# Hybrid encoder block on one core: the first four key tiles projected together behind a run-up of ten matmuls, the first weight chunk and the last store in halves

## The chip, the core and the metric

The kernel runs on one core of a Trainium2 chip. A core has five engines, each with its own instruction list, which it works through in order: TensorE (PE in the profile) multiplies matrices, VectorE (DVE) and ScalarE (ACT) do elementwise work and reductions and can read the accumulators, GpSimd (POOL) does elementwise work on the main on-chip memory, and SyncE (SP) issues transfers. DMA engines move data between the large memory and the on-chip memory. The engines wait for one another through semaphores. PE writes its results to accumulators in a small memory of its own (PSUM). The metric is the time of one execution in microseconds on the device.

## The reference

One layer of an encoder on 1024 positions of 1024 channels, in float32. The parts that matter here come first:

```python
h = rms_norm(x, norm1_g[l])
z = h @ w_in[l]
a, gate, q, k, v = jnp.split(z, splits, axis=-1)
conv_out = conformer_conv(a, gate, ...)            # a * sigmoid(gate), depthwise conv of width 31, LayerNorm, SiLU
q = rms_norm(q.reshape(B, S, N_HEADS, HEAD_DIM), q_norm_g[l])
k = rms_norm(k.reshape(B, S, N_HEADS, HEAD_DIM), k_norm_g[l])
attn_out = neighbourhood_attention(q, k, v, rpb[l])
x = x + jnp.concatenate([conv_out, attn_out], axis=-1) @ w_out[l]
h = rms_norm(x, norm2_g[l])
x = x + (jax.nn.silu(h @ w_gate[l]) * (h @ w_up[l])) @ w_down[l]
```

The key part of `z` is 512 channels wide, eight heads of 64; `a` and `gate` are 512 channels each.

## The kernel before

Every matrix product is made exact enough with three products of a faster kind. An operand is split into a high part (a rounded copy) and a low part (what the rounding left), and `mac` (L110) runs three matmuls into one accumulator: high by high (L112), then the two mixed products (L113 and L114). A weight chunk of 128 x 1024 is split by `split` (L103): ACT casts the high part (L104), and DVE or POOL subtracts for the low part (L108). Weights come through a ring of three raw buffers (`R`); `issue` starts the transfer of the next chunk on SP, `take` and `take_parts` split one, the latter in parts that the caller orders. The first four chunks are `wk0` to `wk3`, the key weights, each holding two of the eight K steps. Then come the GLU chunks, `ag10` (gate, channel block 0) and `ag00` (its value) first. The low parts of the `wk` chunks are made by DVE where `take_parts` is called, those of the `ag` chunks by POOL.

The activations come as transposed x in pieces `xt` of two K steps. `h_split` scales one K step by `norm1_g` and splits it into `hT`; for the first half of the positions (tiles 0 to 3 of 128 positions) it works on 256 columns at a time, `FIRST` for tiles 0 and 1 and `SECOND` for tiles 2 and 3. The factor of the RMS norm is not applied there: it is a number for each position, computed from x itself (`load_x`) by `stats1`, and multiplied in later. `stats1` of an even tile squares and sums on ACT, of an odd tile on DVE; both end with a square root on ACT and a reciprocal on DVE.

The key projection: tiles 0 and 1 are projected together, K step by K step, as the chunks arrive, with the splits of the next pair of K steps between them. The `SECOND` splits follow, then `stats1` of tiles 0 and 1, then tile 2 alone (`project`, 24 matmuls), `stats1` of tiles 2 and 3, the split of `ag10` (`take(1, False)`), and tile 3 alone. Each finished tile goes through `head_post`: a square on ACT, a sum over each head on DVE, a square root on ACT, and the scaling on DVE (`head_sq`, `head_scale`). Then PE transposes the result (`head_T`, L390) and ACT copies it to `kT` (L397). Work of this kind waits in `pend` until the next tile's matmuls have been written out, so it runs beside them; the transposes wait in `woven`, from which one entry is taken after each K step. After the key tiles PE transposes the four factors to a row (`r_rows`, L289), and `glu_step` follows for the gate and value of channel block 0.

The order on each engine is the order in which the program writes the instructions; no scheduler moves them. There are four accumulators of 512 columns for the projections (`mm`) and two for transposes (`tp`).

At the end the down projection finishes its four last tiles one after the other. For each, DVE adds the accumulator to a partial result (L1203) and ACT issues the store (`store`, L1180), 256 KB each.

Of the kernel before, what the change touches and what calls it, by code (L numbers as in the profile page):

```python
# [9 lines left out]
OP = mybir.AluOpType  # L10
PSUM = bass.MemoryType.PSUM

P = 128
D = 1024
S = 1024
KB = D // P
# [51 lines left out]
def build(ctx, tc, a):  # L68
    nc = tc.nc
    pe, act, dve, pool = nc.tensor, nc.scalar, nc.vector, nc.gpsimd  # L70
# [5 lines left out]
    def T(tag, shape, bufs, name, dt=F32):  # L76
        return sb.tile(shape, dt, tag=tag, bufs=bufs, name=name)

    def G(name, dt=F32):
        return T("G", [P, 1024], 22, name, dt)  # L80

    def R(name):
        return T("R", [P, 1024], 3, name)

    def H(name, dt=F32):
        return T("H", [P, 4096], 6, name, dt)

    def ST(name, dt=F32):
        return T("st", [P, 512], 5, name, dt)

    def SM(name, n=8):
        return T("sm", [P, 8], 16, name)[:, :n]

    def mm(name):
        return ps.tile([P, 512], F32, tag="mm", bufs=4, name=name)

    def tp(name):
        return ps.tile([P, 512], F32, tag="tp", bufs=2, name=name)
# [11 lines left out]
    def mac(acc, l, r, start, stop):  # L110
        (lh, ll), (rh, rl) = l, r
        pe.matmul(acc, lh, rh, start=start, stop=False, skip_group_check=True)  # L112
        pe.matmul(acc, lh, rl, start=False, stop=False, skip_group_check=True)  # L113
        pe.matmul(acc, ll, rh, start=False, stop=stop, skip_group_check=True)  # L114


    woven = []
# [16 lines left out]
    def issue():  # L134
        if pos[0] < len(chunks):
            src, name, _, _ = chunks[pos[0]]
            raws[pos[0]] = R(name + "r")
            d = raws[pos[0]]
            if len(src.shape) == 3:
                d = d.rearrange("p (k m) -> p k m", k=src.shape[1])  # L140
            nc.sync.dma_start(d, src)
            pos[0] += 1

    def take(n=1, ahead=True):
# [32 lines left out]
    wn = {n: [] for n in range(3)}  # L177
# [29 lines left out]
    hT = [[H(f"hT{h}{w}", F32R).rearrange("p (k s) -> p k s", s=512) for w in range(2)] for h in range(2)]  # L207
    x_t, xr = {}, {}
    FIRST, SECOND, ALL = slice(0, 256), slice(256, 512), slice(0, 512)

    def load_x(t):
        x_t[t] = G(f"x{t}")
        nc.sync.dma_start(x_t[t], a["x"][t * P:(t + 1) * P, :])

    def load_xt(h, kp, sl):
        if (h, kp) not in xr:
            xr[h, kp] = G(f"xt{h}{kp}").rearrange("p (k s) -> p k s", s=512)
        nc.sync.dma_start(xr[h, kp][:, :, sl], a["xt"][h, kp][:, :, sl])

    for kp in range(4):  # L220
        load_xt(0, kp, FIRST)
        if kp < 3:
            issue()
    ones = ST("ones")[:, :P]
    ident = T("ident", [P, P], 1, "ident")
    par = T("par", [P, 146], 1, "par")
# [7 lines left out]
    warm = SM("warm", 1)  # L234
    act.activation(warm, eps, AF.Sqrt)
    pool.memset(ones, 1.0)
    pool.affine_select(ident, ones, pattern=[[-1, P]], compare_op=OP.is_equal, fill=0.0,
                       base=0, channel_multiplier=1)
    qgs = T("qgs", [P, 1], 1, "qgs")
# [16 lines left out]
    def h_split(h, k, sl):  # L256
        src = xr[h, k // 2][:, k % 2, sl]
        hi, lo = [w[:, k, sl] for w in hT[h]]
        act.activation(hi, src, AF.Copy, scale=g1[:, k:k + 1])
        dve.scalar_tensor_tensor(lo, src, g1[:, k:k + 1], hi.bitcast(F32), OP.mult, OP.subtract)  # L260
# [15 lines left out]
    def stats1(t):  # L276
        ss, scale = (bn_sum if t % 2 else sq_sum)(t)
        sd = SM(f"sd1{t}", 1)
        act.activation(sd, ss, AF.Sqrt, bias=eps, scale=scale)
        dve.reciprocal(r1[:, t:t + 1], sd)  # L280
# [11 lines left out]
    def nat(n, t):  # L292
        z = mm(f"z{n}{t}")
        h, o = divmod(t * P, 512)
        for k in range(KB):
            mac(z, [q[:, k, o:o + P] for q in hT[h]],
                [q[:, (k % 2) * 512:(k % 2) * 512 + 512] for q in wn[n][k // 2]], k == 0, k == KB - 1)
            weave()
        return z
# [56 lines left out]
    def pump(n):  # L356
        for _ in range(n):
            if not next(conv, False):
                return
# [4 lines left out]
    def head_sq(n, t, z):  # L364
        sq, ss = ST(f"sq{n}{t}"), SM(f"s{n}{t}")
        r = r1[:, t:t + 1]
        if n == 1 and t < 4:
            act.activation(sq, z, AF.Square, scale=r)
            dve.tensor_reduce(ss, sq.rearrange("p (h d) -> p h d", d=HD), mybir.AxisListType.X, OP.add)
        else:  # L370
            for h in range(NH):
                act.activation(sq[:, h * HD:(h + 1) * HD], z[:, h * HD:(h + 1) * HD], AF.Square, scale=r,  # L372
                               accum_out=ss[:, h:h + 1])
        sd = SM(f"d{n}{t}")
        act.activation(sd, ss, AF.Sqrt, bias=eps, scale=1.0 / HD)
        return sd

    def head_scale(n, t, z, sd):
        r = SM(f"r{n}{t}")
        dve.reciprocal(r, sd)  # L380
        dve.tensor_scalar(r, r, r1[:, t:t + 1], None, op0=OP.mult)
        zn = ST(f"zn{n}{t}")
        dve.tensor_tensor(zn.rearrange("p (h d) -> p h d", d=HD), z.rearrange("p (h d) -> p h d", d=HD),
                          r[:, :, None].to_broadcast([P, NH, HD]), OP.mult)
        return zn
# [21 lines left out]
    pend = []  # L407
# [10 lines left out]
            pump(n_taps)  # L418
        side()

    def head_post(n, t, z):
        def f(n_taps):
            sd = head_sq(n, t, z)
            pump(2)
            zn = head_scale(n, t, z, sd)
            pump(1)
            woven.extend([lambda: None] * 7)
            woven.append(lambda: head_T(n, t, zn))
        return f

# [70 lines left out]
    def project(n, t, post):  # L501
        z = nat(n, t)
        step(post(n, t, z))

    zs = [mm(f"z1{t}") for t in range(2)]
    for kp in range(4):
        parts = []
        take_parts(parts, 2, dve)
        for j in range(2):
            h_split(0, 2 * kp + j, FIRST)  # L510
            parts[j]()
        if kp == 0:
            for q in range(4):
                load_xt(0, q, SECOND)
            load_x(0)
            load_x(1)
        if kp == 2:
            load_x(2)
            load_x(3)
        for j in range(2):  # L520
            for t in range(2):
                k = 2 * kp + j
                mac(zs[t], [q[:, k, t * P:(t + 1) * P] for q in hT[0]],
                    [q[:, j * 512:(j + 1) * 512] for q in wn[1][kp]], k == 0, k == KB - 1)
    for k in range(KB):
        h_split(0, k, SECOND)
    stats1(0)
    stats1(1)
    pend.extend(head_post(1, t, zs[t]) for t in range(2))
    project(1, 2, head_post)  # L530
    stats1(2)
    stats1(3)
    take(1, False)
    for q in range(4):
        load_xt(1, q, ALL)
    project(1, 3, head_post)
    for t in range(4, 8):
        load_x(t)
    take(1)
# [222 lines left out]
    def rows(ap, t):  # L762
        rh, cb = divmod(t, 4)
        return ap.rearrange("(h i w) d -> h i w d", h=2, w=GW)[rh, :, cb * 16:cb * 16 + 16, :]
# [231 lines left out]
    for t in range(8):  # L996
        for n in range(KB):
            woven.append(lambda fs=beside.get(t, {}).get(n, ()): [f() for f in fs])
        acc = mm(f"pk{t}")
# [10 lines left out]
    gt, bank, sl, u2, late = {}, {}, {}, {}, []  # L1010
# [131 lines left out]
    for n, (i, p) in enumerate(products):  # L1142
        if i == 0 and p in NEXT:
            s_weave(NEXT[p])
        acc = product(i, p)
# [32 lines left out]
    def store(p, t, w):  # L1178
        tok, d = {"m2": (0, 0), "m3": (0, 1), "m4": (1, 0), "m7": (1, 1)}[p]
        (nc.scalar if p == "m4" else nc.sync).dma_start(  # L1180
            rows(a["out"], 4 * tok + t)[:, :, d * 512:(d + 1) * 512], w)

    def quarter(w, o, t):
        return w[:, o + t * 512:o + t * 512 + 512]

    def finish(p, t):
        acc = (GA if p in ("m1", "m2", "m7", "m4") else GB)[t]
        if p == "m1":
            if t == 0:
                om["m1"] = H("om1")  # L1190
            (dve.tensor_copy, act.copy)[t % 2](quarter(om["m1"], 2048, t), acc)
        elif p == "m2":
            dve.tensor_tensor(res[p, t], acc, res[p, t], OP.add)
            store(p, t, res[p, t])
        elif p == "m6":
            if t == 0:
                om["u"] = H("ou")
            dve.tensor_tensor(quarter(om["u"], 0, t), acc, quarter(om["m1"], 2048, t), OP.add)
        elif p == "m5":
            dve.tensor_tensor(quarter(om["u"], 2048, t), acc, quarter(om["m1"], 2048, t), OP.add)  # L1200
        else:
            w = {"m7": quarter(om["u"], 2048, t), "m3": quarter(om["m1"], 2048, t), "m4": quarter(om["u"], 0, t)}[p]
            dve.tensor_tensor(w, acc, w, OP.add)  # L1203
            store(p, t, w)

    def add_res(p, t):
        w = {"m7": quarter(om["u"], 2048, t), "m3": quarter(om["m1"], 2048, t), "m4": quarter(om["u"], 0, t)}[p]
# [8 lines left out]
    for s, p in enumerate(SEQ):  # L1216
        for k in range(QF - 2):
            n = s * QF + k
# [34 lines left out]
```

## Time and profile before

| | |
|---|---|
| median of 3 runs | 1070.03 us (1069.66 to 1070.52) |
| profiled execution, its own time | 1070.39 us |
| span of that execution | 1068.6 us |
| PE busy | 1048.0 us (98%) |
| DVE, ACT, POOL busy | 704.9, 451.3, 383.2 us |
| moved by DMA | 144.06 MB, mean 135 GB/s |

The profile is one execution. Times in it count from the start of the span. A row of the timeline gives start, duration, engine, line, operation, what is written and read, shape, and in square brackets the idle time of the engine before it with what ended it. Matmuls are pipelined, so the duration of one is longer than the distance from one start to the next; the distance is what a matmul costs. A wait is put down to the last event that ended it. In the windows each row gives, for a stretch, the busy time of each engine with the count of its instructions, then the granted clock, the mean busy share of the DMA engines and the GB/s moved.

### The profile page before, as it was taken

The numbers are of one execution on the slowest core, as the hardware profiler recorded it, in microseconds if no ns is written. First come the engines' busy times: TensorE is split into PE (matmuls) and PEld (weight loads), VectorE is DVE, ScalarE is ACT, GpSimd is POOL, SyncE is SP. The second block draws the span as 40 slices with busy tenths as digits, with TensorE's granted clock in tenths as the row PEclk, the third lists the DMA queues.
The fourth block names the chain that finished last, engine by engine and source line by source line (L and its number), as shares of the span: only waits on it lengthen the run. The fifth ranks groups of instructions, "written<-read, shape, count | busy, mean of one in ns | idle before, by whom it ended". The sixth has DMA issues, their size and how long they took to land.

```text
span 1068.6 us, 14069 instructions
## 1 busy us (share of the span) xinstructions
PE 1048.0 (98%) x5068; PEld 849.4 (79%) x5068; DVE 704.9 (66%) x1071; ACT 451.3 (42%) x987; POOL 383.2 (36%) x301
## 2 busy tenths in 40 slices
PE   7999999989999999999999999999999999999997
PEld 6788888866667888788888888888888888888886
DVE  6778997885775347766556465564655567858873
ACT  6455357725775424542322323223232344433441
POOL 0136665513562301435444554445544300002310
PEclk9999999999999999999999999999999999999999
DMA  9426781244413422132322322333232597633641
GB/s 336 158 51 221 225 251 40 75 150 137 152 62 131 164 80 82 37 107 90 128 98 84 134 99 89 109 107 109 81 129 79 179 333 276 207 98 116 216 131 41
DMA packets 68245, 144.06 MB, mean 135 GB/s; under 512 B 12496, under 2 KB 21200, under 8 KB 67536
## 3 DMA queue, kind: packets, MB, share of 16 engines
q1 hardware_dynamic: 66336, 139.95, 38.8%
q10 hardware_dynamic: 1840, 3.22, 0.9%
q8 instruction: 40, 0.66, 0.3%
q14 instruction: 29, 0.24, 0.1%
HBM read 103.99 MB, written 44.76 MB: 139 GB/s over the span
## 4 chain that ended last, share of the span: by engine, by line
PE 89%; DVE 6%; issue 1%; ACT 1%; DMA 1%; POOL 0%; SPq 0%; DVEq 0%; POOLq 0%; ACTq 0%
PE B L113 5%; PE B L114 5%; PE B L112 5%; PE D L114 4%; PE D L112 4%; PE D L113 4%; PE A L112 3%; PE A L114 3%; PE A L113 3%; DVE cv L319 3%; PE gl L114 3%; PE gl L112 3%; PE gl L113 3%; PE z L112 2%; PE z L113 2%; PE z L114 2%
## 5 line engine op out<-in xcount | busy, mean ns | idle before, releaser
L319 DVE SCALAR_TENSOR_TENSOR cv<-u,par,cv 128x1009 f32<-128x1009 f32 (+14 forms) x92 | 117.5, 1277 | 2.5
L345 POOL TENSOR_TENSOR pa<-pa,pr 128x1022 f32<-128x1022 f32 (+5 forms) x24 | 57.5, 2398 | 51.3 <-ACT pr L344 42.8
L104 ACT CAST op<-sr 128x512 fp32r<-128x512 f32 x77 | 47.7, 619 | 51.2 <-PE B2d L114 23.3
L108 DVE TENSOR_TENSOR op<-sr,op 128x512 fp32r<-128x512 f32 x77 | 57.6, 748 | 15.9 <-ACT op L104 15.8
L1036 DVE TENSOR_TENSOR g<-B,g 128x512 f32<-128x512 f32 x22 | 15.2, 691 | 79.0 <-PE B L114 79.0
L1208 POOL TENSOR_TENSOR ou<-ou,resm 128x512 f32<-128x512 f32 x8 | 13.2, 1662 | 142.9 <-DMA resm<-xd 142.9
L1045 ACT ACTIVATE D<-D 128x512 f32<-128x512 f32 x22 | 12.8, 582 | 113.1 <-DVE D L1044 113.1
L1031 DVE TENSOR_TENSOR u<-B,g 128x512 f32<-128x512 f32 x22 | 15.2, 690 | 62.5 <-PE B L114 62.5
L104 ACT CAST op<-wd 128x512 fp32r<-128x512 f32 x66 | 40.9, 619 | 31.6 <-DVE wd L1123 18.3
L108 DVE TENSOR_TENSOR op<-wd,op 128x512 fp32r<-128x512 f32 x66 | 51.7, 783 | 2.4 <-ACT op L104 0.9
L633 POOL TENSOR_SCALAR e<-e,rs 128x288 f32<-128x288 f32 (+1 forms) x64 | 34.2, 548 | 52.8 <-DVE rs L631 42.3
L889 DVE TENSOR_TENSOR ts<-gu,ts 128x512 f32<-128x512 f32 x44 | 51.0, 1159 | 0.8
L1034 ACT ACTIVATE A<-A 128x512 f32<-128x512 f32 x20 | 11.6, 582 | 76.3 <-PE A L114 76.3
L626 ACT ACTIVATE e<-e,mx 128x288 f32<-128x288 f32 (+1 forms) x64 | 36.2, 568 | 11.4 <-DVE mx L624 11.4
L624 DVE CUSTOM_DVE_ANT_0 e<-s,tab 128x288 f32<-128x288 f32 (+1 forms) x64 | 29.9, 504 | 6.7 <-PE s L611 6.4
L889 DVE TENSOR_TENSOR ts<-gu 128x512 f32<-128x512 f32 x22 | 33.5, 1524 | 0.0
L611 PE MATMUL s<-kT,qT 64*128 64x288 f32 (+1 forms) x128 | 28.1, 499 | 4.6 <-DVE mx L624 4.6
L642 PEld LDWEIGHTS p<-ident,e 128*96 128x96 f32 (+1 forms) x192 | 20.1, 133 | 15.0 <-issue 10.4
L372 ACT ACTIVATE sq<-z,r 128x64 f32<-128x64 f32 x96 | 28.6, 334 | 2.2 <-PE z L114 2.2
L642 PE MATMUL p<-ident,e 128*96 128x128 f32 (+1 forms) x192 | 27.6, 280 | 0.6 <-DVE pT L647 0.6
L658 PE MATMUL o<-pT,vw 96*64 96x128 f32 (+1 forms) x384 | 28.0, 281 | 0.0
L344 ACT ACTIVATE pr<-u,par 128x1022 f32<-128x1022 f32 (+5 forms) x24 | 27.0, 1137 | 1.6 <-ACT vs L403 1.6
(1039 smaller groups left out, 3455.0 us busy)
## 6 DMA issues: line engine op xcount, KB each, us to landing
gu<-in_gu SPq DMA_DIRECT2D x44, 512.0 KB
sr<-sd SPq DMA_DIRECT2D x77, 256.0 KB
sd<-sd SPq DMA_DIRECT2D x22, 512.0 KB
wd<-in_wd SPq DMA_DIRECT2D x44, 256.0 KB
sd<-g SPq DMA_DIRECT2D x33, 256.0 KB
x<-in_x SPq DMA_DIRECT2D x16, 512.0 KB
xd<-x SPq DMA_DIRECT2D x8, 512.0 KB
resm<-xd SPq DMA_DIRECT2D x16, 256.0 KB
```

Of the source, the lines that this page charges most:

```text
L104: act.copy(hi, src)
L108: eng.tensor_tensor(*[w[..., sl] for w in (lo, src, hi.bitcast(F32))], OP.subtract)
L112: pe.matmul(acc, lh, rh, start=start, stop=False, skip_group_check=True)
L113: pe.matmul(acc, lh, rl, start=False, stop=False, skip_group_check=True)
L114: pe.matmul(acc, ll, rh, start=False, stop=stop, skip_group_check=True)
L319: dve.scalar_tensor_tensor(acc[:, o], uc[:, i], dwk[:, c, t:t + 1], acc[:, o], OP.mult, OP.add)
L345: pool.tensor_tensor(pa[:, o], pa[:, o], pr[:, o], OP.add)
L624: dve.tensor_tensor_reduce(out=e[:, hh], in0=ss[hh], in1=tab[rh, cb][2 * hp + hh], scale=-1.0, scalar=3.0e38, op0=OP.add, op1=OP.min, accu ...
L626: act.activation(e[:, hh], e[:, hh], AF.Exp, bias=mx, scale=-1.0, accum_out=rs[:, hh:hh + 1])
L633: pool.tensor_scalar(es[i][:, hh], es[i][:, hh], rs[:, hh:hh + 1], 1.0, op0=OP.mult, op1=OP.mult)
L642: pe.transpose(pt[:m, g * P:(g + 1) * P], es[i][:, hh, g * m:(g + 1) * m], ident)
L889: dve.tensor_tensor(o, l, r, OP.subtract)
```

## The change

- All four accumulators are taken at once: tiles 0 to 3 of the keys are projected together. For the first three chunks the order is K step by K step over the four tiles; for the last chunk each tile does both its K steps, so that the tiles finish one after the other.
- The `SECOND` halves of the transposed x are issued directly behind each `FIRST` half and its chunk, and split beside them. x tiles 0 and 1 are issued in the second round, 2 and 3 in the third.
- `stats1` of all four tiles comes before the last round's matmuls, and `head_post` of tiles 0, 1 and 2 is written out among these matmuls, with a lag of two K steps instead of seven for the transposes. Tile 3's follows in the first `glu_step`. The split of `ag10` now stands behind all this, and that of `ag00` directly behind it.
- Ten matmuls of a 128 x 128 tile of ones with itself are written ahead of the first projection, into an accumulator for transposes that nobody reads.
- The first weight chunk's transfer is issued as two transfers of 512 columns.
- The last tile's final addition and store are done in two halves of 256 columns, the first stored from SP, the second from ACT.

```diff
@@ issue
-            nc.sync.dma_start(d, src)
+            for q in (0, 1) if name == "wk0" else (slice(None),):
+                sl = slice(q * 512, q * 512 + 512) if name == "wk0" else q
+                nc.sync.dma_start(d[:, sl], src[:, sl])
@@ the first loads
         load_xt(0, kp, FIRST)
         if kp < 3:
             issue()
+        load_xt(0, kp, SECOND)
...
     pool.memset(ones, 1.0)
+
+    run_up = tp("up")
+    for _ in range(10):
+        pe.matmul(run_up[:, :P], ones, ones, start=True, stop=True)
@@ head_post
-    def head_post(n, t, z):
+    def head_post(n, t, z, lag=7):
...
-            woven.extend([lambda: None] * 7)
+            woven.extend([lambda: None] * lag)
@@ the key projection
-    zs = [mm(f"z1{t}") for t in range(2)]
+    zs = [mm(f"z1{t}") for t in range(4)]
+
+    def four(kp, j, t):
+        k = 2 * kp + j
+        mac(zs[t], [q[:, k, t * P:(t + 1) * P] for q in hT[0]],
+            [q[:, j * 512:(j + 1) * 512] for q in wn[1][kp]], k == 0, k == KB - 1)
+
     for kp in range(4):
         parts = []
         take_parts(parts, 2, dve)
         for j in range(2):
             h_split(0, 2 * kp + j, FIRST)
             parts[j]()
-        if kp == 0:
-            for q in range(4):
-                load_xt(0, q, SECOND)
-            load_x(0)
-            load_x(1)
-        if kp == 2:
-            load_x(2)
-            load_x(3)
         for j in range(2):
-            for t in range(2):
-                k = 2 * kp + j
-                mac(zs[t], [q[:, k, t * P:(t + 1) * P] for q in hT[0]],
-                    [q[:, j * 512:(j + 1) * 512] for q in wn[1][kp]], k == 0, k == KB - 1)
-    for k in range(KB):
-        h_split(0, k, SECOND)
-    stats1(0)
-    stats1(1)
-    pend.extend(head_post(1, t, zs[t]) for t in range(2))
-    project(1, 2, head_post)
-    stats1(2)
-    stats1(3)
+            h_split(0, 2 * kp + j, SECOND)
+        if kp in (1, 2):
+            load_x(2 * kp - 2)
+            load_x(2 * kp - 1)
+        if kp == 3:
+            for t in range(4):
+                stats1(t)
+        for q in range(8):
+            j, t = divmod(q, 4) if kp < 3 else (q % 2, q // 2)
+            four(kp, j, t)
+            if kp == 3 and j == 1 and t < 3:
+                head_post(1, t, zs[t], 2)(4)
+    pend.append(head_post(1, 3, zs[3], 2))
     take(1, False)
     for q in range(4):
         load_xt(1, q, ALL)
-    project(1, 3, head_post)
     for t in range(4, 8):
         load_x(t)
     take(1)
@@ finish, last product
-            dve.tensor_tensor(w, acc, w, OP.add)
-            store(p, t, w)
+            for o, q in ((0, nc.sync), (256, nc.scalar)) if (p, t) == ("m4", 3) else ((None, None),):
+                if q is None:
+                    dve.tensor_tensor(w, acc, w, OP.add)
+                    store(p, t, w)
+                else:
+                    sl = slice(o, o + 256)
+                    dve.tensor_tensor(w[:, sl], acc[:, sl], w[:, sl], OP.add)
+                    q.dma_start(rows(a["out"], 4 + t)[:, :, sl], w[:, sl])
```

## The prediction

> **What bounds the kernel now.** I read the page's busy times and chain first, then PE's waits, then the order of time on each engine for the first 60 us and the last 10. Busy time and chain say that PE is the bound:
>
> ```profile
> span 1068.6 us, 14069 instructions
> PE 1048.0 (98%) x5068; PEld 849.4 (79%) x5068; DVE 704.9 (66%) x1071; ACT 451.3 (42%) x987; POOL 383.2 (36%) x301
> PE 89%; DVE 6%; issue 1%; ACT 1%; DMA 1%; POOL 0%; SPq 0%; DVEq 0%; POOLq 0%; ACTq 0%
> ```
>
> So a gain or a loss has to show as PE time. PE's waits (engine, line, what it waited for: total, times, longest) name where it stands still:
>
> ```profile
> PE z L112 <- ACT wk0h L104: 6.5, 1, 6.5
> PE s L611 <- DVE mx L624: 4.6, 1, 4.6
> PE gl L114 <- POOL ag10l L108: 0.6, 1, 0.6
> ```
>
> The first is the front, which the change attacks; the third is the gate behind the work that is regrouped. The timeline of PE (start, duration, instruction) around both:
>
> ```profile
> 6.50 0.79 PE L112 MATMUL z<-wk0h,hT 128*128 128x512 f32 x1 [6.50 <-ACT wk0h L104]
> 7.22 0.80 PE L113 MATMUL z<-wk0l,hT 128*128 128x512 f32 x1
> 10.80 0.48 PE L112 MATMUL z<-wk0h,hT 128*128 128x512 f32 x1
> 11.12 0.40 PE L113 MATMUL z<-wk0l,hT 128*128 128x512 f32 x1
> 11.35 0.40 PE L114 MATMUL z<-wk0h,hT 128*128 128x512 f32 x1
> ...
> 30.42 0.40 PE L114 MATMUL z<-wk3h,hT 128*128 128x512 f32 x1
> 30.66 0.60 PE L390 MATMUL zt<-ident,zn 128*128 128x128 f32 x4
> 31.09 0.60 PE L289 MATMUL rb<-ident,r 128*128 128x128 f32 x4
> 31.45 0.48 PE L112 MATMUL gl<-hT,ag10h 128*128 128x512 f32 x1
> 31.77 0.39 PE L113 MATMUL gl<-hT,ag10h 128*128 128x512 f32 x1
> 32.80 0.50 PE L114 MATMUL gl<-hT,ag10l 128*128 128x512 f32 x1 [0.65 <-POOL ag10l L108]
> ```
>
> Nine matmuls start from 7.22 to 10.80 and take 3.90 us until 11.12, where the pace is then 0.227 each (11.12 to 11.35): about 1.9 us lost to a slow start. At 32.80 PE passes the gate: the low half of the first GLU weight chunk, which POOL makes. ACT and POOL show how the gate comes about:
>
> ```profile
> 4.27 0.51 ACT L259 ACTIVATE hT<-xt,par 128x256 fp32r<-128x256 f32 x1 [1.57 <-DMA xt<-in_xt]
> 5.83 0.62 ACT L104 CAST wk0h<-wk0r 128x512 fp32r<-128x512 f32 x1 [1.04 <-DMA wk0r<-in_qkv]
> 8.75 0.62 ACT L104 CAST wk1h<-wk1r 128x512 fp32r<-128x512 f32 x1 [0.77 <-DMA wk1r<-in_qkv]
> 13.67 0.62 ACT L104 CAST wk3h<-wk3r 128x512 fp32r<-128x512 f32 x1 [0.95 <-DMA wk3r<-in_qkv]
> 15.12 3.31 ACT L259 ACTIVATE hT<-xt,par 128x256 fp32r<-128x256 f32 x8
> 18.33 1.01 ACT L273 ACTIVATE j<-x 128x1024 f32<-128x1024 f32 x1
> 21.90 0.67 ACT L368 ACTIVATE sq<-z,r 128x512 f32<-128x512 f32 x1
> 23.33 0.30 ACT L375 ACTIVATE d<-s,eps 128x8 f32<-128x8 f32 x1 [0.75 <-DVE s L369]
> 25.48 0.30 ACT L375 ACTIVATE d<-s,eps 128x8 f32<-128x8 f32 x1 [1.28 <-DVE s L369]
> 25.69 1.01 ACT L273 ACTIVATE j<-x 128x1024 f32<-128x1024 f32 x1
> 29.26 1.04 ACT L104 CAST ag10h<-ag10r 128x1024 fp32r<-128x1024 f32 x1
> 30.38 2.37 POOL L108 TENSOR_TENSOR ag10l<-ag10r,ag10h 128x1024 fp32r<-128x1024 f32 x1 [29.03 <-DMA xt<-in_xt]
> ```
>
> ACT runs its list in order: statistics of x tiles 0 and 1 (18.33 to 21.90, 3.57 us), heads of key tiles 0 and 1 (21.90 to 25.69), statistics 2 and 3 (25.69 to 29.26, 3.57), the cast ag10h (29.26), then POOL's subtraction 1.12 later, and PE 2.42 after that. The chunk itself is no matter: what the cast waits for is its turn. All this is covered today by PE's 48 matmuls of key tiles 2 and 3; only 0.65 us is not.
>
> **The change, part by part.** First the front. wk0 in halves: ACT can cast its first half when 256 KB less have come. At the 333 GB/s of the row below that is about 0.75 us, bounded by 5.83 (no earlier) and 4.78 (ACT free). I take 5.1, and with 0.67 from cast to matmul as before (5.83 to 6.50) PE starts at 5.8.
>
> ```profile
> 0.78 0.21 POOL L236 MEMSET ones<- 128x128 f32 x1 [0.29 <-POOLq L1243]
> 4.00:5.00 1.00, 0.00 (x0) 0.00 (x0) 0.18 (x1) 0.51 (x1) 0.00 (x0) 1.00 0.97 333
> 20.00:21.00 1.00, 1.00 (x6) 0.84 (x5) 1.00 (x2) 0.00 (x0) 0.00 (x0) 1.00 1.04 414
> ```
>
> The ten matmuls on ones wait for the memset (0.99). The trace has none like them; a transposition of the same size is 0.11 us (30.66 to 31.09 is four), a slow 128x512 matmul 0.43, so they take 1.1 to 4.3 us and end by 5.3, on an idle PE: no cost. If they ran past 5.8 PE would start later by the excess. Their gain is 0 to 1.9 us of slow matmuls; I take it whole.
>
> The four tiles: 96 matmuls, as before. 5.8, then 0.72 to the second (6.50 to 7.22), then 95 steps of 0.227: key tile 0 is done at 24.0, tile 2 at 26.7, tile 3 at 28.1, where before it was 30.65. The x transposes' second halves now go past wk1, wk2 and wk3 on SP. wk1 comes behind 256 KB more, 0.6 us at 414 GB/s: 9.4, and its first matmul is due at 11.9, after 24 of them. wk3 comes behind 1 MB more, 2.5 us: 16.2, due at 22.8. Both are covered; a lost cover would cost the excess alone.
>
> Then the gate. In the changed program ACT's list is: all four statistics, heads 0, 1, 2, cast ag10h. The statistics start after wk3's split: 16.2 plus 1.45 (13.67 to 15.12) plus two splits of 0.41 is 18.5, about the 18.33 of before, which I keep. They also need x0, which SP now issues behind ag10: 512 KB, 1.27 us at 414 GB/s, so up to 19.6 if it had landed just in time. Four statistics are 2 x 3.57, with no overlap of the pairs, since each pair ends on ACT with a square root that waits for DVE: 25.5. That is later than key tile 0 (24.0), so the early finish of PE buys nothing here. Three heads: two took 3.79 (21.90 to 25.69), a third adds 2.15 (23.33 to 25.48): 5.94. Cast at 31.4, POOL at 32.5, PE through the gate at **35.0**. Bounds: 24.0 instead of 25.5 gives 33.5; x0 late gives 36.2.
>
> So the gate opens 2.2 us later than at 32.80. Behind it everything queues on PE in order: the rest of the GLU, and the transposes of all four key tiles, of which one set (0.43 us) stood ahead of the gate before, at 30.66: +0.43. ag00, POOL's next split, is due 24 matmuls on and is hidden. Of the waits that PE has after the gate only the 4.6 us is large, and it hangs on DVE work that starts from the GLU's results, so what PE loses at the gate passes to the end in full.
>
> New: PE has nothing to do from 28.6 (tile 3 and the four rb transposes) to ag10h's end at 32.5, and again from about 33 to 35.0. What a pause of that size does stands in the trace once:
>
> ```profile
> 237.00 1.32 PE L611 MATMUL s<-kT,qT 64*128 64x288 f32 x2 [4.61 <-DVE mx L624]
> 238.25 0.79 PE L112 MATMUL z<-w20h,hT 128*128 128x512 f32 x1
> 242.68 0.58 PE L113 MATMUL z<-w21l,hT 128*128 128x512 f32 x1
> 243.10 0.39 PE L114 MATMUL z<-w21h,hT 128*128 128x512 f32 x1
> 243.33 0.39 PE L112 MATMUL z<-w22h,hT 128*128 128x512 f32 x1
> ```
>
> After 4.61 us without work the eleven steps from 238.25 to 243.10 take 4.85 us instead of 2.5: 2.35 lost. After the 0.65 us at 32.80 nothing is lost. Pauses of 3.9 and 2 us with two matmuls between lie nearer the first; between 0 and 2.35 I take 2.2.
> The Trainium skill (TensorE: Matmul & The Clock Gate, Part 1) has it that a window of about 3.4 us without work halves the clock until a busy window has passed; the windows run free, so 3.9 us does not always hold a whole one. The trace agrees with the halving (0.43 against 0.227); by the page the price is 2.2 or 0, and the sum 1074.3 or 1072.1.
>
> Last the final store. Its rows (windows: PE, PEld, DVE, ACT, POOL busy, clock, share of DMA, GB/s):
>
> ```profile
> 1058.86 4.69 ACTq L1180 DMA_DIRECT2D out_dram<-ou  x4
> 1063.00:1064.00 1.00, 0.00 (x0) 0.00 (x0) 0.00 (x0) 0.00 (x0) 0.00 (x0) 1.00 0.51 190
> 1066.00:1067.00 1.00, 0.00 (x0) 0.00 (x0) 0.00 (x0) 0.00 (x0) 0.00 (x0) 0.50 0.48 178
> ```
>
> ACT's queue alone keeps the DMA engines half busy and drains four stores of 256 KB until about 1067. 128 KB on SP's queue instead shortens that backlog by 0.7 us at 178 GB/s; with packets half as long it could be nothing. I take 0.5. The adds in halves are hidden by the backlog.
> The Trainium skill (Trainium Kernel Development and Optimization, Key Constraints) says that issuing from several engines only saves issue time; no row shows two store queues at once. By it the tail gains nothing and the sum is 1074.8.
>
> **Sum** against the profiled execution (1070.39): +2.2 gate, +0.43 transposes, +2.2 slow matmuls, -0.5 tail: +4.3, 1074.7. The median of the runs is 0.36 lower than that execution, so 1074.3.
>
> **The rivals.**
> No slow spell: the gate opens late but PE keeps its pace. For it: the pauses are shorter than 4.61 and broken by two matmuls. +2.1: 1072.1.
> The gate hardly moves: statistics are done by 24.0, because they take less when consecutive or because x comes early. Then 33.5, +0.7 and +0.43, the pause is 2.5 us and costs nothing, -0.5: 1070.7. Against it: each square root waits for DVE, and x0 has more ahead of it.
> Faster: the front's gain passes. If the cast of ag10h did not sit behind the heads, the GLU would run on at 28.6 and its third matmul at 29.1, 3.7 us early; with +0.43 and -0.5 that is 1066.3. It decides from the point where the gate opens before 30.8, 2.1 us earlier than now with +0.43 and -0.5 about even. The rows speak against it: even from key tile 0's end at 24.0 three heads, the cast and POOL need 9.5 us.
> The run-up does nothing: PE starts slow, tile 0 is done at 25.9, tile 3 at 30.0; the gate opens at 35.4 after a pause of 2.9 us: +2.6, +0.43, 0 to +2.2, -0.5, so 1072.6 to 1074.8. This lies within the forecast's own span.
>
> **How the numbers follow.** A measurement here tells about 0.2% (2.1 us) from no change: slower begins at 1072.2. Late gate with slow spell, or with the run-up failing: 0.63, by its bounds 1072.6 to 1076.6 (x0 late by 1.2, the dearest slow spell, no tail gain). No slow spell: 0.20, and the bound of 0.2% halves it. Gate hardly moves: 0.13, same. Faster: 0.04. So slower 0.73, same 0.23, faster 0.04. The range leaves out the faster case and the far ends: 1070.7 to 1076.4.
>
> **What would show it.** In the profile of the changed kernel: the first matmul on wk0h near 5.8 and steps of 0.227 soon after; tile 3 done near 28; the wait of PE for ag10h and then ag10l, some 6 us together, where 0.65 stood; ag10h's cast near 31.4, behind the third head's square root; 0.43 us steps after the gate; and the last bytes some half a microsecond sooner after the last matmul. Wrong would be: ag10h cast before 29, or a GLU that follows the key tiles without a pause.

## The result, and the profile after

The changed kernel is slower: 1076.63 us as the median of 6 runs (1075.61 to 1077.43), against 1069.94 us for the kernel before, also 6 runs, on the same chip. The ratio is 1.0061, with a 95% interval of [1.0050, 1.0071]. That is 2.3 us above the forecast of 1074.3 and 0.23 us above the range; the direction was the forecast one. The profiled execution took 1076.57 us, next to the median, with a span of 1074.8 us.

The page's head and PE's waits (engine, line, what it waited for: total, times, longest):

```profile
span 1074.8 us, 14114 instructions
PE 1055.3 (98%) x5088; PEld 855.1 (80%) x5088; DVE 708.2 (66%) x1072; ACT 451.5 (42%) x987; POOL 383.1 (36%) x301
```

```profile
PE s L616 <- DVE mx L629: 4.6, 1, 4.6
PE gl L112 <- ACT ag10h L104: 3.3, 1, 3.3
PE gl L114 <- POOL ag10l L108: 1.4, 1, 1.4
PE up L243 <- POOL ones L239: 1.0, 1, 1.0
```

The wait of 6.5 us for `wk0h` at the front is gone; 1.0 us on the ones has taken its place, and the ten matmuls (in float32 the profile counts them as 20) fill most of the rest. What is new sits at the gate: 3.3 us for the high part of `ag10` and 1.4 us for its low part, where 0.65 us stood. The 4.6 us on DVE's `mx` is unchanged. PE's busy time rose by 7.3 us: 4.6 of it is the ten matmuls themselves, which ran while PE would have been idle, and most of the rest is matmuls at half pace. The timeline of PE around the front and the gate:

```profile
1.04 4.63 PE L243 MATMUL up<-ones 128*128 128x128 f32 x20 [1.04 <-POOL ones L239]
6.04 0.79 PE L112 MATMUL z<-wk0h,hT 128*128 128x512 f32 x1 [0.37 <-ACT wk0h L104]
7.36 0.63 PE L114 MATMUL z<-wk0h,hT 128*128 128x512 f32 x1
7.79 0.63 PE L112 MATMUL z<-wk0h,hT 128*128 128x512 f32 x1
...
10.35 0.42 PE L112 MATMUL z<-wk0h,hT 128*128 128x512 f32 x1
10.61 0.40 PE L113 MATMUL z<-wk0l,hT 128*128 128x512 f32 x1
...
30.14 0.60 PE L296 MATMUL rb<-ident,r 128*128 128x128 f32 x4
34.04 0.61 PE L112 MATMUL gl<-hT,ag10h 128*128 128x512 f32 x1 [3.30 <-ACT ag10h L104]
34.45 0.63 PE L113 MATMUL gl<-hT,ag10h 128*128 128x512 f32 x1
36.49 0.79 PE L114 MATMUL gl<-hT,ag10l 128*128 128x512 f32 x1 [1.41 <-POOL ag10l L108]
37.08 0.63 PE L112 MATMUL gl<-hT,ag10h 128*128 128x512 f32 x1
...
40.34 0.78 PE L112 MATMUL gl<-hT,ag10h 128*128 128x512 f32 x1
40.92 0.48 PE L113 MATMUL gl<-hT,ag10h 128*128 128x512 f32 x1
41.24 0.39 PE L114 MATMUL gl<-hT,ag10l 128*128 128x512 f32 x1
41.47 0.40 PE L112 MATMUL gl<-hT,ag10h 128*128 128x512 f32 x1
```

Three readings. The first matmuls step by 0.43 until 10.35 in spite of 4.63 us of run-up. The gate opens at 36.49. Behind it the steps are 0.43 again until 40.92. ACT and POOL say why the gate is at 36.49:

```profile
17.06 0.62 ACT L104 CAST wk3h<-wk3r 128x512 fp32r<-128x512 f32 x1 [0.61 <-DMA wk3r<-in_qkv]
19.59 1.03 ACT L280 ACTIVATE j<-x 128x1024 f32<-128x1024 f32 x1 [0.18 <-DMA x<-in_x]
23.43 1.03 ACT L280 ACTIVATE j<-x 128x1024 f32<-128x1024 f32 x1
27.02 0.67 ACT L375 ACTIVATE sq<-z,r 128x512 f32<-128x512 f32 x1
32.75 0.30 ACT L382 ACTIVATE d<-s,eps 128x8 f32<-128x8 f32 x1 [1.28 <-DVE s L376]
32.96 1.03 ACT L104 CAST ag10h<-ag10r 128x1024 fp32r<-128x1024 f32 x1
34.07 2.36 POOL L108 TENSOR_TENSOR ag10l<-ag10r,ag10h 128x1024 fp32r<-128x1024 f32 x1 [32.72 <-ACT ag10h L104]
```

The order is the predicted one: four statistics, three heads, cast, subtraction. From the first head (27.02) to PE's passage (36.49) it is 9.47 us; the prediction had 9.5. The start of the heads is what differs.

An account by the two profiles, at the start of the last addition on DVE: it stood at 1062.21 before and stands at 1068.43 now, 6.22 us later. Of that the gate gives 36.49 − 32.80 = 3.69, the set of transposes that moved behind it 0.43, and the half-paced matmuls 2.12: from the gate to the eleventh matmul from it, with one set of transposes between, it is 4.98 us here (36.49 to 41.47), and 2.86 us for the same work at full pace in the filler kernel below (35.80 to 38.66). Together that is 6.24. Behind the addition nothing has changed: to the end of the span it was 6.39 us and is 6.37. The last stores (windows: PE, PEld, DVE, ACT, POOL busy, granted clock, DMA share, GB/s):

```profile
1068.91 0.60 SPq L1215 DMA_DIRECT2D out_dram<-ou  x1
1069.27 0.61 ACTq L1215 DMA_DIRECT2D out_dram<-ou  x1
1071.00:1072.00 1.00, 0.00 (x0) 0.00 (x0) 0.00 (x0) 0.00 (x0) 0.00 (x0) 0.97 0.51 187
1072.00:1073.00 1.00, 0.00 (x0) 0.00 (x0) 0.00 (x0) 0.00 (x0) 0.00 (x0) 0.50 0.54 187
```

With two queues at work the share of the DMA engines is still about 0.5 and the rate 187 GB/s, the numbers of one queue before.

### The profile page after: what moved, and what is told of

The parts are those of the page before. It is cut to its first block, busy times and chain, and to the rows that moved or that the text cites. A ratio compares the mean times of both kernels' runs of the same rounds, so it can differ in the third digit from the quotient of the medians.

```text
span 1074.8 us, 14114 instructions
## 1 busy us (share of the span) xinstructions
PE 1055.3 (98%) x5088; PEld 855.1 (80%) x5088; DVE 708.2 (66%) x1072; ACT 451.5 (42%) x987; POOL 383.1 (36%) x301
## 4 chain that ended last, share of the span: by engine, by line
PE 89%; DVE 5%; issue 2%; ACT 1%; DMA 1%; SPq 0%; POOL 0%; DVEq 0%; POOLq 0%; ACTq 0%
PE B L113 5%; PE B L114 5%; PE B L112 5%; PE D L112 4%; PE D L114 4%; PE D L113 4%; PE A L112 3%; PE A L114 3%; PE A L113 3%; PE gl L114 3%; DVE cv L326 3%; PE gl L112 3%; PE gl L113 3%; PE z L112 2%; PE z L113 2%; PE z L114 2%
## 5 line engine op out<-in xcount | busy, mean ns | idle before, releaser
L631 ACT ACTIVATE e<-e,mx 128x288 f32<-128x288 f32 (+1 forms) x64 | 36.2, 568 | 11.4 <-DVE mx L629 11.4
L616 PE MATMUL s<-kT,qT 64*128 64x288 f32 (+1 forms) x128 | 28.1, 500 | 4.6 <-DVE mx L629 4.6
```

What stands on the lines that cost most here:

```text
L631: act.activation(e[:, hh], e[:, hh], AF.Exp, bias=mx, scale=-1.0, accum_out=rs[:, hh:hh + 1])
```

## The experiments

The theory is the prediction's: the turn of `ag10`'s cast on ACT sets the gate, and the pause at the gate slows PE behind it. The rivals: the run-up or the front set something, the key tiles' new order costs by itself, or the loads are late for reasons of their own.

**Undo one thing, the turn of the cast.** In the changed kernel `take(1, False)` goes between the statistics of tiles 1 and 2:

```diff
             for t in range(4):
                 stats1(t)
+                if t == 1:
+                    take(1, False)
...
-    take(1, False)
```

> The changed kernel with one call moved: ag10 is split between the statistics of tiles 1 and 2 instead of behind the third head. Theory (the gate: ag10h's place in ACT's list made the 3.7 us and, through the pause, the slow spell): POOL is done with ag10l near 27, the third GLU matmul starts near 31.5 instead of 36.5, no pause over 1 us on PE, no 0.43 us steps behind it; time 1.3 us less than before at the gate, +0.43 for the transposes: about 1069, 7.5 us less than the changed kernel. Rival (the regrouping itself costs, whatever ACT's order): within 1 us of 1076.6.

It took 1070.38 us (1069.63 to 1070.86, 10 runs), ratio to before 1.0002 [0.9993, 1.0011]. The gate, first, and then the one wait that is new (timeline):

```profile
24.28 2.40 POOL L108 TENSOR_TENSOR ag10l<-ag10r,ag10h 128x1024 fp32r<-128x1024 f32 x1 [22.93 <-ACT ag10h L104]
31.40 0.40 PE L114 MATMUL gl<-hT,ag10l 128*128 128x512 f32 x1
42.06 0.63 PE L397 MATMUL zt<-ident,zn 128*128 128x128 f32 x4 [1.20 <-DVE zn L390]
```

POOL has the low part at 26.68, almost 5 us before PE wants it, PE passes without a wait, and 6.3 us of the 6.7 are back from one moved line. So the new order of the key tiles is not what costs the 6.7 us; the cast's turn on ACT is. The gate now opens 1.40 us earlier than before the change (31.40 against 32.80), yet the time is only level: 0.43 goes to the transposes that moved, and 1.20 to a wait that the late gate had covered. The heads come later now, and PE reaches the transposes of key tile 3 before DVE has scaled it.

**Take the run-up away.** The changed kernel without the ten matmuls on ones:

```diff
-    run_up = tp("up")
-    for _ in range(10):
-        pe.matmul(run_up[:, :P], ones, ones, start=True, stop=True)
```

> The changed kernel without the ten matmuls on ones. Theory (they do nothing here: the matmuls after them started slow all the same, and the gate hides the front): first matmul near 6.0, slow steps until about 10.4, gate near 36.5, 1076.6 within 0.5. Rival (they shorten the slow start): more slow steps, key tile 0 done later than the 27.0 at which its head starts, up to 1 us more, 1077.5.

1075.77 us (1075.70 to 1077.45, 4 runs), ratio 1.0060 [1.0043, 1.0076]: no difference from the changed kernel. The first matmul came at 6.39 and the steps were slow until 12.40, so the key tiles ended later; PE then waited 2.6 us instead of 3.3 for the cast, and the gate opened at 36.87. A slow front is not quite free, though: here the first head on ACT waited 0.36 us for key tile 0.

**Fill the pause.** 22 unused matmuls of 128 x 512 stand between the key tiles and the gate, in an accumulator that nobody reads; what the kernel computes is unchanged.

```diff
+    pad = tp("pad")
+    for i in range(22):
+        pe.matmul(pad, hT[0][0][:, i % 8, :P], wn[1][i % 8 // 2][0][:, :512], start=True, stop=True)
```

> The changed kernel with 22 matmuls of 128x512 on operands that lie ready, written between the rb transposes and the GLU, into an accumulator that nobody reads: they fill the pause of 30.6 to about 35.6 and leave the gate. Theory (the pause makes the slow spell): the gate stays at 36.5 within 0.3, steps of 0.227 behind it, 2.1 us less than the changed kernel, 1074.5. Rival (the slow steps have another cause): 0.43 us steps remain behind the gate, 1076.6.

1074.05 us (1073.46 to 1075.68, 4 runs), ratio 1.0041 [1.0026, 1.0056], 2.6 us under the changed kernel by the medians and 2.1 by the ratios to the kernel before. Its timeline, and a window of it:

```profile
35.80 0.50 PE L114 MATMUL gl<-hT,ag10l 128*128 128x512 f32 x1 [1.50 <-POOL ag10l L108]
36.14 0.39 PE L112 MATMUL gl<-hT,ag10h 128*128 128x512 f32 x1
36.37 0.40 PE L113 MATMUL gl<-hT,ag10h 128*128 128x512 f32 x1
...
38.66 0.40 PE L112 MATMUL gl<-hT,ag10h 128*128 128x512 f32 x1
36.00:38.00 2.00, 2.00 (x12) 1.64 (x12) 2.00 (x2) 0.70 (x2) 2.00 (x1) 1.00 0.60 213
```

Behind the gate the steps are 0.23 at once and the granted clock stays at 1.00. The slow steps are a matter of the pause, and their price of about 2 us is measured. In this execution the gate was also 0.7 earlier than in the changed kernel's, with `wk3` cast at 15.74; 2.1 and 0.7 make a little more than the 2.6.

**The front alone.** The kernel before, with `wk0` in halves and the run-up, and nothing else:

```diff
+            for q in (0, 1) if name == "wk0" else (slice(None),):
+                sl = slice(q * 512, q * 512 + 512) if name == "wk0" else q
+                nc.sync.dma_start(d[:, sl], src[:, sl])
...
+    run_up = tp("up")
+    for _ in range(10):
+        pe.matmul(run_up[:, :P], ones, ones, start=True, stop=True)
```

> The kernel before with wk0 in halves and the ten matmuls on ones, and nothing else. Theory (before, too, the gate's time comes from ACT's list, which starts with statistics at 18.3 and not from PE): PE starts near 6.0, the gate stays at 32.8 within 0.3, 1070.0 within 0.5. Rival (what PE gains at the front passes to the end): 0.5 to 2.3 us less, 1067.7 to 1069.5.

1069.78 us (1068.99 to 1070.55, 10 runs), ratio 0.9998 [0.9988, 1.0007]: nothing. Timeline of PE:

```profile
5.58 0.49 PE L112 MATMUL z<-wk0h,hT 128*128 128x512 f32 x1 [0.62 <-ACT wk0h L104]
6.88 0.40 PE L112 MATMUL z<-wk0h,hT 128*128 128x512 f32 x1
7.11 0.39 PE L113 MATMUL z<-wk0l,hT 128*128 128x512 f32 x1
...
10.51 0.49 PE L112 MATMUL z<-wk1h,hT 128*128 128x512 f32 x1 [1.31 <-ACT wk1h L104]
...
32.97 0.50 PE L114 MATMUL gl<-hT,ag10l 128*128 128x512 f32 x1 [1.27 <-POOL ag10l L108]
```

Here the run-up worked: PE starts 0.92 us earlier than before and steps by 0.23 from 6.64 on. All of it is spent waiting, above all 1.31 us for `wk1` and 1.27 at the gate (0.65 before), which opens at 32.97 as it did at 32.80. A gain in front of a gate that ACT sets is worth nothing.

**The early cast and later transposes.** To the first experiment is added a lag of seven K steps for the transposes of key tile 3 ("T3"):

```diff
-    pend.append(head_post(1, 3, zs[3], 2))
+    pend.append(head_post(1, 3, zs[3], 7))
```

> The kernel with ag10 split early, and the transposes of key tile 3 seven K steps later instead of two. Theory (the early split gave back 1.4 us at the gate, and 1.2 us of it went into the wait of these transposes for zn13): no wait over 0.3 us on PE from the key tiles to the second GLU pair, 1.2 us less than the kernel with ag10 early, about 1069.0, and 1.0 us less than before. Rival (the 1.2 us returns as another wait, for instance for the second half of hT or for ag00): 1070.2, as before.

1069.07 us (1067.33 to 1069.36, 11 runs), ratio 0.9982 [0.9973, 0.9991]: now it is 0.2% faster than the kernel before. The wait at T3 is gone; PE's waits name the next one, the accumulator of key tile 0, which the GLU needs and which DVE's scaling has not yet released:

```profile
PE gl L112 <- DVE zn L390: 1.1, 1, 1.1
```

The same without the run-up:

> The same without the ten matmuls on ones. Here PE is busy without a pause from the first matmul to the second GLU pair, so what the front costs must show in the time. Theory (the run-up sometimes speeds up the first matmuls and sometimes does not, so it is worth about half of the 1.9 us): 0.5 to 1.5 us more than with it. Rival (worth nothing, as in the changed kernel's profile): equal within 0.4.

1068.65 us (1067.76 to 1069.34, 11 runs), ratio 0.9985 [0.9976, 0.9994]. PE starts at 6.45 and steps slowly until 11.18, reaches the GLU at 31.18 instead of 30.72 (its statistics, too, began 0.65 us earlier), and finds the accumulator free: no wait for `zn`. Times with and without the run-up cannot be told apart, so the theory's 0.5 to 1.5 us did not come. Most of what the front saves, that wait takes; the rest, 0.46 us at the GLU, is smaller than what the low clock makes of a later pause (last section).

**Whole pieces.** The changed kernel loads the transposed x for the first half in pieces of 256 columns; here the pieces from the second K-step pair on are loaded whole, which makes three transfers fewer on SP ahead of `wk3`:

```diff
-        load_xt(0, kp, FIRST)
+        load_xt(0, kp, FIRST if kp == 0 else ALL)
...
-        load_xt(0, kp, SECOND)
+        if kp == 0:
+            load_xt(0, kp, SECOND)
```

> The changed kernel with the pieces of the transposed x for the second, third and fourth pair of K steps loaded whole (512 KB) instead of in two halves: the same bytes in the same order in three transfers fewer. Theory A (wk3 came late because its issue waited until 9.6 for an earlier transfer to land, the many small ones having taken the places): wk3's issue moves to about 8.2, its cast from 17.1 to about 16, statistics and gate about 1 us earlier, up to 1 us less. Theory B (the bytes ahead of it set it): cast at 17 within 0.5, gate at 36.5 within 0.5, 1076.6.

1076.16 us (1074.50 to 1077.95, 4 runs), ratio 1.0053 [1.0038, 1.0067]. In its profile `wk3` was cast at 15.77, against 17.06; but the filler kernel, with small pieces, had 15.74. In this execution the gate opened at 35.12 instead of 36.49, and it took 1074.50 us, 2.1 less than the profiled execution of the changed kernel; but of the three others two took 1077.49 and 1077.95, so the median shows no gain. Both kernels ran once more, on one chip:

> The changed kernel as it is, on one chip with the next. Both theories: 1076.6 within 0.6; it is there for the comparison with whole pieces.

> The changed kernel with whole hT pieces from the second K step on. Theory A: about 1 us less than the changed kernel of the same chip, so 1075.6, with wk3's cast about 1 us ahead of that of the changed kernel. Theory B: equal to it within 0.5, and wk3's cast anywhere between 15.7 and 17.1 in both.

The changed kernel took 1075.95 us (ratio 1.0061 [1.0048, 1.0075]), whole pieces 1075.71 (1.0057 [1.0044, 1.0069]), 5 runs each: no difference in time that these runs can tell. The casts of `wk3` stand on the side of the pieces: 15.63 here against 16.62, and between 15.63 and 16.03 in all four profiled executions with whole pieces, against 15.74 in one and 16.29 to 17.06 in six of those with small ones. So the small pieces delay `wk3` in most executions, and still the medians do not differ. The gates of the two (changed kernel first, then whole pieces; timeline, and windows with the granted clock third from the end):

```profile
36.52 0.80 PE L114 MATMUL gl<-hT,ag10l 128*128 128x512 f32 x1 [1.22 <-POOL ag10l L108]
40.82 0.39 PE L112 MATMUL gl<-hT,ag10h 128*128 128x512 f32 x1
32.00:34.00 2.00, 0.00 (x0) 0.00 (x0) 1.56 (x5) 1.21 (x3) 0.00 (x0) 0.72 0.93 369
38.00:40.00 2.00, 2.00 (x8) 1.51 (x7) 2.00 (x2) 0.00 (x0) 1.35 (x2) 0.58 0.54 209
```

```profile
35.70 0.80 PE L114 MATMUL gl<-hT,ag10l 128*128 128x512 f32 x1 [1.73 <-POOL ag10l L108]
40.92 0.40 PE L112 MATMUL gl<-hT,ag10h 128*128 128x512 f32 x1
32.00:34.00 2.00, 0.73 (x2) 0.30 (x2) 1.65 (x4) 2.00 (x3) 0.73 (x1) 1.00 0.79 313
40.00:42.00 2.00, 2.00 (x8) 1.59 (x8) 0.30 (x1) 0.63 (x1) 0.00 (x0) 0.80 0.56 211
```

With whole pieces the gate is 0.82 us earlier, but the eleventh matmul from it starts at 40.92 against 40.82. In the changed kernel's execution the clock had gone to half at 32.9, while PE was idle, and was back at 39.7; with whole pieces it went to half at 34.0 and stayed there until 40.8. In this execution the gain passed into a low clock that lay later over the work. The cast itself did not gain the whole of `wk3`'s 1 us either: with a slow front (PE was slow until 10.11) the first head waited 0.70 us for key tile 0.

**Two queues.** The kernel before, with the four last stores taking turns between ACT and SP:

```diff
-        (nc.scalar if p == "m4" else nc.sync).dma_start(
+        (nc.scalar if p == "m4" and t % 2 == 0 else nc.sync).dma_start(
```

> The kernel before with the last four stores shared out: tiles 0 and 2 from ACT's queue, tiles 1 and 3 from SP's, each whole. Theory A (my prediction's: one queue drains at about 178 GB/s and a second adds to that): from the start of the last addition to the end of the span 5.0 us or less instead of 6.4, 1.4 us less. Theory B (the stores share what limits them whichever queue issues them, which is why the halves gained 0.02 us): 6.4 within 0.3, 1070.0.

1069.71 us (1068.88 to 1070.96, 10 runs), ratio 0.9994 [0.9984, 1.0003]. From the last addition to the end it is 6.32 us (6.39 before), and the window shows one queue's share and rate:

```profile
1064.00:1065.00 1.00, 0.00 (x0) 0.00 (x0) 0.00 (x0) 0.00 (x0) 0.00 (x0) 1.00 0.53 180
```

**The early cast, the later transposes and whole pieces together.**

> The kernel with the early cast of ag10 and the later T3, and the hT pieces of all key tiles but the first pair's first K step loaded whole. Theory A (the number of pieces delays wk3): wk3 is cast about 1 us earlier than 16.95, the statistics begin about 1 us earlier, PE's wait of 1.1 us for zn shrinks to near nothing, and the time is about 1068.1, 1 us under the kernel with pieces (1069.07). Theory B (wk3's landing is set by bytes, and its scatter is from run to run): 1069.1 within 0.5, and a wait for zn of about 1 us.

1068.29 us (1067.20 to 1069.47, 11 runs), ratio 0.9985 [0.9976, 0.9994]. `wk3` was cast at 15.80, as the first theory had it, but then the statistics waited 1.70 us for x tile 0 and began at 19.84, and the wait for `zn` was 1.8 us. So in this execution the earlier `wk3` was worth nothing: the x tile was next in line. It is not always: in the profile of the next version, whose loads are the same, `wk3` was cast at 16.03, the statistics began at 18.35 without a wait, and the wait for `zn` was 0.57 us.

**The last stores from POOL**, on top of that version:

```diff
-        (nc.scalar if p == "m4" else nc.sync).dma_start(
+        (nc.gpsimd if p == "m4" else nc.sync).dma_start(
...
-            for o, q in ((0, nc.sync), (256, nc.scalar)) if (p, t) == ("m4", 3) else ((None, None),):
+            for o, q in ((0, nc.gpsimd), (256, nc.gpsimd)) if (p, t) == ("m4", 3) else ((None, None),):
```

> The version with the early cast, the later T3 and whole pieces, with the four last tiles' stores all issued from POOL instead of ACT and SP. Theory A (each of these stores, whose pattern has 8 outer rows, goes to 8 of the 16 DMA engines, the same 8 from ACT and from SP; from POOL the 8 would take turns between the two halves): the DMA share rises above 0.6 and the rate above 220 GB/s in the last microseconds, the backlog goes and the last addition is followed by the end of the span in about 5.3 us instead of 6.3, so 1067.3. Theory B (the stores share a limit that has nothing to do with which engines they use): share about 0.5, 140 to 190 GB/s, and the time equal or later by POOL's own issue, 1068.3 to 1070.

1069.58 us (1068.35 to 1072.48, 12 runs), ratio 1.0000 [0.9992, 1.0009], 1.3 us more than the version it was built on. Windows:

```profile
1062.00:1063.00 1.00, 0.00 (x0) 0.00 (x0) 0.00 (x0) 0.00 (x0) 0.00 (x0) 1.00 0.63 185
1063.00:1064.00 1.00, 0.00 (x0) 0.00 (x0) 0.00 (x0) 0.00 (x0) 0.00 (x0) 0.50 0.66 226
```

The share does rise above 0.6 and one window reaches 226 GB/s, as the first theory wanted, but the tail from the last addition (1059.81) to the end (1066.7) is 6.89 us, longer than 6.48 in the version it was built on. That is 0.4 of the 1.3 us; where the rest comes from is not shown. The traces do not name the DMA engine of a transfer, so the cause of the half share stays open; no way of issuing that was tried shortens the tail.

## Why the prediction was right or wrong

**The gate: the mechanism right, the size too small.** The cast behind four statistics and three heads was the cause: moving the cast alone took 6.3 us back. The term was +2.2 and measured +3.69. The step that failed is "The statistics start after wk3's split ... about the 18.33 of before, which I keep". They started at 19.59: `wk3` was cast at 17.06 instead of 16.2 and x tile 0 added 0.18; most of the other 0.2 is the step from the 18.5 that had been worked out down to 18.33. A further quarter of a microsecond came between the two pairs of statistics (19.59 to 23.43, 3.84 instead of 3.57). Together that is the 1.5 us by which the term was too small. Of two values for that start, 18.33 and 19.6, the one without a new wait was kept, although the new order had put 1 MB in front of `wk3` and `ag10` in front of the x tile. The other would have been met by chance: it was worked out for a late x tile, and most of the delay was `wk3`'s. The parts shift from execution to execution. In the repetition of the changed kernel the start was 0.85 late (19.18), the two pairs took 7.88 instead of 7.14 with waits for x tiles of 0.15 on ACT and 0.35 on DVE, and the gate came at 36.52, almost where it was.

**The slow steps: the mechanism right, the size in part luck.** 2.2 forecast, 2.12 in the profile, and the filler shows that they belong to the pause. But with the same late gate the loss, counted in the same way, was 1.30 us without the run-up, 1.44 in the repetition, and 1.54 and 2.36 with whole pieces; the forecast had no term for what decides that (last section). The rival without a slow spell is refuted in both profiled executions of the changed kernel.

**The transposes: right**, 0.43, seen again in the first experiment's account.

**The tail: wrong.** −0.5 was taken and −0.02 came. The step that failed is "128 KB on SP's queue instead shortens that backlog by 0.7 us at 178 GB/s": the two queues together moved no more than one did, 141 to 187 GB/s in the full windows against 160 to 190 before. The sentence cited from the Trainium skill (Trainium Kernel Development and Optimization, Key Constraints), that several issuing engines save only issue time, was the better guide: 6.39 us with one queue, 6.37 and 6.32 with two.

**The front: the step failed in this execution and it did not matter.** The gain of the run-up was taken whole; the profiled execution had none of it (slow until 10.35), so tile 3 ended at 30.14 and not at 28.1, and PE waited 4.7 us at the gate instead of some 6. The prediction said that an early finish buys nothing here because ACT's statistics end later, and the runs show that: in the repetition the run-up did work, tile 3 ended at 28.86, and the gate opened at 36.52 all the same; without the run-up it opened only 0.38 later.

The sum in the profiles: 3.69 + 0.43 + 2.12 − 0.02 = 6.2, against 4.3. Of the 1.9 between them 1.5 is the gate and 0.5 the tail, less 0.1 at the slow steps. The rest of the 2.3 against the medians is the distance of the profiled executions from their medians. The dearest case of the range already had the statistics start at 19.6, so its gate at 36.2 was only 0.3 too early. But its 1076.6 is on the scale of the profiled execution; added to the forecast of 1074.3, the same terms (1.2 for the x tile, 0.15 for the dearest slow spell, 0.5 for the tail) give 1076.15. The measured median lies 0.5 above that, and 0.2 above the end that was set.

Against the rival on the other side, the case "faster", the condition that was named, the gate open before 30.8, was nearly met by the first experiment (31.40). By the prediction's account that gate would have brought 1.0 us (−1.40 + 0.43, without a gain at the tail), and the time was level. What the account left out is the next wait, 1.20 us at T3.

## What to carry to other kernels

When work is regrouped, read the list of the engine that opens the next stage and ask what now stands ahead of the opening instruction: here one cast, left behind four statistics and three heads on ACT, cost 6.3 us although PE's own work had become shorter. Time saved ahead of such a gate is worth nothing until the gate moves, and when it moves the next wait (T3, then an accumulator, then an x tile) takes part of it. For a transfer that is moved behind others, take the later of the two landing times into the sum, not the old one. And when two kernels differ by less than a microsecond, look at the clock behind each pause of PE before giving the difference to the edit.

## What the runs showed of the hardware

**The low clock comes in spells of 3.4 or 6.8 us.** In the records the granted clock goes to 0.50 and back. The spell lasted 6.8 us in the kernel before (around the pause that ended at 237.00), 6.8 in the changed kernel (34.28 to 41.11), 6.8 in its repetition (32.87 to 39.70) and 6.8 with whole pieces, but 3.4 without the run-up (36.33 to 39.74) and 3.4 at the front of the first experiment (7.32 to 10.73). The stretches at full clock between two changes are whole multiples of 3.41 us too, 23.89 in the changed kernel (10.39 to 34.28). The Trainium skill (TensorE: Matmul & The Clock Gate, Part 1) states windows of 3413 ns that run free of the kernel; one and two of them are the lengths seen. The Trainium skill asks there for a window without work before the clock falls. That is more than the runs ask for: with whole pieces the clock fell at 34.0, and the 3.4 us before that held a set of transposes' end and two matmuls, with 2.56 us idle; at the front of the first experiment a pause of 1.62 us was enough. Pauses of 1.3 to 1.8 us elsewhere (front alone, 1.31; the filler kernel, 1.50; early cast, later T3 and whole pieces, 1.8) brought no fall.

**What a pause costs depends on where the spell lies.** The cost is about half of what is left of the spell when work comes. From the gate to its end 2.9, 3.2, 3.4, 4.6 and 5.1 us of it were left (without the run-up, the repetition, whole pieces, the changed kernel, whole pieces again), and the losses, counted to the eleventh matmul as above, were 1.30, 1.44, 1.54, 2.12 and 2.36. The pause of 4.6 us that ends at 237.00 in the kernel before stands in every profile of this case (its end lies between 234.9 and 243.3), each time with a spell of 6.8 us. From its end to the last addition it was 824.24 to 825.54 us in the 14 profiles; less half of what was left of the spell (3.9 to 6.7 us) it is 822.14 to 822.31 in all of them. So this one pause, whose length hardly changes, makes up to 1.3 us of difference between two executions. It is why the later T3 without the run-up, 0.27 us behind its twin with the run-up when that pause ended, made the last addition 0.46 us ahead of it.

**A run-up does not always bring the pace.** The same ten matmuls, 3.9 to 4.6 us long, were followed by slow steps until 10.35 in the changed kernel and 10.11 with whole pieces, and by steps of 0.23 from 6.64 with the front alone and from 7.20 in the repetition. The clock record of each trace begins with a change to full clock, and in the changed kernel that is at 10.39, where the slow steps end; the windows show 1.00 for the time before it, so there the distance of the starts must be read instead. Of the ten profiles with the run-up eight have that first change between 3.91 and 6.83 and two at 10.10 and 10.39; of the four without it, all between 10.98 and 12.44. In one of the eight, the first experiment, the clock fell again at 7.32. What decides was not found.
